# A decoder layer on one core: Y rows loaded by token halves, head values two to a PSUM bank, merged rows' low parts on VectorE, and three gate columns left at the first logits

## The chip, the cores and the metric

The kernel runs on one core of a Trainium2 chip. The metric is the device time of one execution in microseconds, lower is better; the time before is the median of three executions. TensorE (PE) multiplies matrices into PSUM banks of 128 x 512 float32 values; VectorE (DVE), ScalarE (ACT) and GpSimd (POOL) move and change data; SyncE (SP) issues most of the DMA transfers.

## The reference, cut to what matters

One layer, 1024 tokens, width 1024, eight heads of 64 in each of two attentions that run side by side. The change touches the sparse attention's output, the gated merge and the start of the output projection.

```python
x = x + 0.5 * swiglu(rms_norm(x, g_ffn1), w1_gate, w1_up, w1_down)      # inner width 2816
h = rms_norm(x, g_mix)
(c_q, k_a, v_a, k_idx, w_idx, q_b, k_b, v_b, gate_a, gate_b) = split(h @ w_in)
# A: sparse attention, each token attends to its 256 best keys by an indexer's score
logits = where(valid, q_a . k_a * HEAD_DIM ** -0.5, -inf)
p = softmax(logits)                                                     # per head
o_lat = p @ v_a                                                         # latent values, 128 wide
y_a = concat over heads of (o_lat @ w_uv[head])                         # value weights, 128 x 64 a head
# B: stick-breaking attention, causal, without softmax
y_b = (exp(log_sigmoid(z) + cumulated log_sigmoid(-z))) @ v_b
merged = sigmoid(gate_a) * (y_a @ w_o_a) + sigmoid(gate_b) * (y_b @ w_o_b)
x = x + merged @ w_out
x = x + 0.5 * swiglu(rms_norm(x, g_ffn2), w2_gate, w2_up, w2_down)
```

## The kernel before

Everything is float32. A product is made of three matmuls of a faster format (`mm3`, L306 to L310): each operand is split into a high part, a rounded copy made by ScalarE, and a low part, the rest, made by a subtraction on VectorE or POOL. Names ending in h and l (`uvh`, `uvl`, `wg7h`, `wout010l`) are such parts; `halve` (L375) puts the high part of a 128 x 512 piece into the first half of a tile and its low part into the second.

The two SwiGLU halves at the ends take most of the time and are not touched. Between them lies a part in which the order of TensorE's, VectorE's, ScalarE's and POOL's work is written out by a planner, `Weave`. Each piece of work is a generator that yields the engine it wants next and what it needs: tiles, marks (named events), free places in a ring of buffers, and a rank. `Weave.run` steps the piece that by a table of costs can begin first, and of those the one with the lowest rank. So a change in one piece moves others. SP's queue takes its transfers strictly in the order in which they were written. Behind the planner's part the order is set by the framework's scheduler.

The pieces that the change touches, in the planner's second stretch:

- `fillers` projects the columns of values, queries and keys, and then the sixteen 128-wide columns of the two gates, 48 matmuls `psf` a column, with weights `wg0` to `wg7` for the last eight. Before the last two but one column in its list it sets the mark "warm", for which `logits` waits. `gate_out` scales the results (with one more instruction on POOL if ScalarE's table is already that of the exponential) and writes them to memory.
- `sparse` loads the value weights (`uvraw`): POOL clears two tiles of 128 x 512, eight transfers of 128 x 64 fill them, ScalarE and POOL make `uvh` and `uvl`.
- `logits`, `logit_out` and `soft`: for each block of 128 queries and each head, TensorE's logits `psL`, VectorE's masking and maximum `mx` (L1907), ScalarE's exponential (L1919) and VectorE's division `e` (L1922). `latent_values` and `latent_products` turn e on TensorE (`pspT`, L1998) and multiply it with the latent values (`pso`).
- `head_values` multiplies pairs of 128-token blocks with the value weights: for four pairs of heads, six matmuls `psya` of 256 columns each, into a bank of the ring `fbank`; `ya_out` makes the parts `yah` (ScalarE, L2037) and `yal` (VectorE, L2039).
- `outputs` and `project`: B's output rows come back from memory in tiles of 128 x 1024 (`ybh0` to `ybh3` and `ybl0` to `ybl3`, 512 KB each) and are multiplied with `w_o_b` (`psob`); one wait stands for all eight tiles. The second token half of A's product (`psoa`) follows. `gate_load` brings the gates, `gated` and `merged` multiply (`o`, L2064 to L2078) and store. The eight Y_b tiles share a ring of 16 (`ht`) with other tiles.

Then, outside the planner: for the first token half A's product `psm` with gates and B's part loaded into tiles of the same ring of 16 (L2147, L2148: eight times two transfers of 256 KB), the product with `w_out` (`psout`, L308 to L310 with weights `wout000` and on), and between its halves `merged` (L2210), which loads the second token half's merged rows `m10` to `m17` and halves them, low parts on POOL (L378). The adds to the residual stream, `x` L2184, are on VectorE.

Of the kernel before, what the change touches and what calls it, by code (L numbers as in the profile page):

```python
# [21 lines left out]
PE, DVE, ACT, POOL, SP = "PE", "DVE", "Activation", "Pool", "SP"  # L22

P = 128
# [7 lines left out]
HD = 64  # L32
# [25 lines left out]
def f32(ap):  # L58
    return ap.bitcast(F32)
# [34 lines left out]
class Weave:  # L94
# [113 lines left out]
    def spawn(self, gen, rank=1, own=None):  # L208
        s = Stream(gen, rank, own or self.own)
        self.streams.append(s)  # L210
        self.step(s)
        return s
# [33 lines left out]
def trunk(ctx, tc, x, positions, g_ffn1, w1_gate, w1_up, w1_down, g_mix, w_in, g_cq, w_uq_a, w_q_idx,  # L246
          g_q_a, g_k_a, w_uv_a, w_o_a, w_o_b, w_out, g_ffn2, w2_gate, w2_up, w2_down, inv_freq, out):
    nc = tc.nc
# [15 lines left out]
    def ht(name, dt=F32R):  # L264
        return hpool[-1].tile([P, 1024], dt, tag="h", name=name, bufs=16)
# [40 lines left out]
    def mm3(ps, ah, al, bh, bl, first, last):  # L306

        nc.tensor.matmul(ps, ah, bh, start=first, stop=False)  # L308
        nc.tensor.matmul(ps, ah, bl, start=False, stop=False)  # L309
        nc.tensor.matmul(ps, al, bh, start=False, stop=last)  # L310
# [62 lines left out]
    HI, LO = slice(0, 512), slice(512, 1024)  # L373

    def halve(t, src, eng=None):  # L375

        nc.scalar.activation(t[:, HI], src, AF.Copy)
        (eng or nc.gpsimd).tensor_tensor(t[:, LO], src, f32(t[:, HI]), op=ALU.subtract)  # L378
        return t
# [398 lines left out]
    ybd = [dram.tile([512, S], F32, name=f"yb{p}d") for p in "hl"]  # L778
# [40 lines left out]
    with tc.tile_pool(name="ring1", bufs=1) as rpool, tc.tile_pool(name="s1", bufs=1) as spool, tc.tile_pool(name="ps1", bufs=1, space=PSUM) as psum:  # L819
        op, raw = ring(rpool)  # L820
        bank = banks(psum, fpsum)
        sums, pair = of(spool, "s", 5, 512), of(spool, "pair", 2, 512, F32R)
        with tc.tile_pool(name="t1", bufs=1, side="right") as tpool, tc.tile_pool(name="c1", bufs=1) as cpool:
            tt, ts = of(tpool, "t", 24, dt=F32R), of(tpool, "ts", 4, dt=F32R)
# [42 lines left out]
            def rows(t):  # L867
                xs.append(fp(tt if t > 3 else ts)(f"x{t}"))
                nc.sync.dma_start(xs[t], x[0, t * P:(t + 1) * P, :])
# [89 lines left out]
        h2, rows = [], []  # L959
# [31 lines left out]
        rows = normed(xs[0:4], "m0", sx)  # L991
# [36 lines left out]
    with ctxf, fp as fpool, psm as psum, tc.manual_schedule(  # L1028
# [174 lines left out]
        def fillers():  # L1203
            yield from proj_v(0)
            for n, (pr, (base, nh_, nl_, sc)) in enumerate(todo):
                if n == 4:
                    yield from proj_v(1)
                if not n % 2:
                    outs = []
                s = feed()  # L1210
                yield PE, s
                for half in range(2):
                    yield PE, fbank
                    ps, cols = yield from fproj(s.parts, half)
                    outs.append(spawn(qk_out(ps, pr, nh_, nl_, sc, cols)))
                give(*s.parts)
                if n % 2:
                    mark(f"qk{pr}", *outs, qkd["kl"], qkd["kh"], qkd["qh"], qkd["ql"])
            outs = []
            for g in gates:  # L1220
                if g == gates[-2]:
                    mark("warm")
                s = feed()
                yield PE, s
                for half in range(2):
                    yield PE, fbank, late(3)
                    ps, cols = yield from fproj(s.parts, half, lambda: late(3))
                    outs.append(spawn(gate_out(ps, g, cols)))
                give(*s.parts)
            mark("gates", *outs)  # L1230
# [638 lines left out]
        def sparse():  # L1869
            c = here["c"] = outputs_of[1] = place("sd", "right")  # L1870
            here["gate"], here["e"] = ring_of(c, "gate", 3, (P, 512)), ring_of(c, "e", 3)

            UV.extend((c("uvh", "uvh", 1, F32R), c("uvl", "uvl", 1, F32R)))
            raws = [here["gate"]("uvraw") for half in range(2)]
            mark("c")
            yield POOL
            for half, raw in enumerate(raws):
                nc.gpsimd.memset(raw, 0.0)
                for h in range(4):
                    nc.sync.dma_start(raw[:, h * P + h % 2 * HD:h * P + (h % 2 + 1) * HD], w_uv_a[0, 4 * half + h])  # L1880
            for half, raw in enumerate(raws):
                cols = slice(half * 512, half * 512 + 512)
                yield ACT, raw
                nc.scalar.activation(UV[0][:, cols], raw, AF.Copy)
                yield POOL, raw, UV[0]
                nc.gpsimd.tensor_tensor(UV[1][:, cols], raw, f32(UV[0][:, cols]), op=ALU.subtract)
                give(raw)
            mark("uv", UV[1])
# [115 lines left out]
            yield PE, *outs  # L2004
            give(*KV)

        ybh, ybl, yah, yal = [], [], [], []

        def head_values():
            yield PE, "gates"  # L2010
            yah.extend(ht(f"yah{p}") for p in range(4))
            yal.extend(ht(f"yal{p}") for p in range(4))
            yield PE, "uv"
            uvh, uvl = UV
            for n in range(NT // 2):
                i = blocks[2 * n] // 2 * 2
                yield PE, f"o{n}"
                cols = slice(i * P, (i + 2) * P)
                outs = []
                for pr in range(4):  # L2020
                    yield PE, fbank
                    bank = fbank("psya")
                    yp = bank[:, 0:256]
                    for e in range(2):
                        h = 2 * pr + e
                        oh, ol = (a[:, (h % 4) * 256:(h % 4 + 1) * 256] for a in OT[i // 2, h // 4])
                        hc = slice(h * P, (h + 1) * P)
                        mm3(yp, uvh[:, hc], uvl[:, hc], oh, ol, e == 0, e == 1)
                    outs.append(spawn(ya_out(bank, yah[pr], yal[pr], cols)))
                for g in range(2):  # L2030
                    give(*OT[i // 2, g])
                mark(f"ya{n}", *outs)

        def ya_out(bank, hi, lo, cols):
            yp = bank[:, 0:256]
            yield ACT, bank
            nc.scalar.activation(hi[:, cols], yp, AF.Copy)  # L2037
            yield DVE, bank, hi
            nc.vector.tensor_sub(lo[:, cols], yp, f32(hi[:, cols]))  # L2039
            give(bank)  # L2040
# [45 lines left out]
        def project(nm, rows, halves, outs):  # L2086

            for d in range(0, ND, 2):
                W = feed()
                yield PE, W  # L2090
                wh, wl = W.parts
                for e in range(2):
                    for half in halves:
                        yield PE, rows[-1][-1], fbank
                        cols = slice(half * 512, half * 512 + 512)
                        ps, r = fbank("ps" + nm), slice((d + e) * P, (d + e + 1) * P)
                        row, to = (ND + d + e, obd[r, cols]) if nm == "ob" else (d + e, md[r, :])
                        coming = spawn(gate_load(row, d + e, half, nm == "oa"))
                        for k in range(4):
                            c = slice((2 * k + e) * P, (2 * k + e + 1) * P)  # L2100
                            mm3(ps, wh[:, c], wl[:, c], rows[0][k][:, cols], rows[1][k][:, cols], k == 0, k == 3)
                            if k < 3:
                                yield PE
                        outs.append(spawn((merged if nm == "oa" else gated)(ps, coming, row, half, to)))
                    if nm == "ob":
                        mark(f"obd{d + e}", *outs[-len(halves):])
                give(*W.parts)

        def outputs():

            yield PE, "gates"
            ybh.extend(ht(f"ybh{p}") for p in range(4))
            ybl.extend(ht(f"ybl{p}") for p in range(4))
            yield SP, "o"
            for p in range(4):
                nc.sync.dma_start(f32(ybh[p]), ybd[0][p * P:(p + 1) * P, :])
                nc.sync.dma_start(f32(ybl[p]), ybd[1][p * P:(p + 1) * P, :])
            yield PE, "c"
            outs = []
            yield from project("ob", (ybh, ybl), range(2), outs)  # L2120
            yield PE, "ya2"
            yield from project("oa", (yah, yal), range(1, 2), outs)

        for g, rank in ((v_loads(), 0), (values(), 0), (sticks(), 1), (head_values(), 2), (latent_values(), 3), (logits(), 4),
                        (hidden_keys(), 1), (latent_queries(), 1), (outputs(), 6)):
# [11 lines left out]
    with tc.tile_pool(name="ring2", bufs=1) as rpool, tc.tile_pool(name="ps6", bufs=1, space=PSUM) as psum:  # L2137
        op, raw = ring(rpool)
        bank = banks(psum)
        with tc.tile_pool(name="m0", bufs=1) as mpool:  # L2140
# [70 lines left out]
            def merged():  # L2211
                for d in range(0, ND, 2):
                    m = raw(f"m1{d}r")
                    nc.sync.dma_start(m.rearrange("p (k f) -> p k f", k=2),
                                      md[d * P:(d + 2) * P, :].rearrange("(k p) f -> p k f", p=P))
                    M1.extend(halve(tt(f"m1{d + q}"), m[:, c]) for q, c in enumerate((HI, LO)))

            project(0, M0, x0, merged)
        sums = of(ctx3.enter_context(tc.tile_pool(name="s2", bufs=1)), "s", 7, 512)
# [76 lines left out]
```

## Time and profile before

| what | value |
| --- | --- |
| median of three executions | 2169.08 us (2166.69 to 2172.35) |
| the profiled execution: its time, its span | 2170.9 us, 2169.1 us |
| mean granted TensorE clock | 0.998 |
| TensorE, VectorE, ScalarE, POOL busy | 98%, 71%, 48%, 42% of the span |
| moved by DMA | 378.89 MB, 174 GB/s of HBM traffic over the span |

In the profile an idle time stands in brackets behind the instruction that it precedes, with what ended it. Two figures are not the same: an idle time is the gap between instructions as recorded, while TensorE's matmuls are issued every 0.23 us (512 columns) and overlap by about 0.16 us, so the delay from start to start is a little longer. The planner's second stretch ends where `psm` begins, at 1411.65 us.

### The profile page before, as it was taken

How to read it: one execution, taken by the hardware profiler on the slowest of the kernel's cores; microseconds unless marked ns; L12 is line 12 of the kernel's file. 1: busy time of each engine (PE TensorE's matmuls, PEld its weight loads, DVE VectorE, ACT ScalarE, POOL GpSimd, SP SyncE). 2: the span in 40 equal slices, each digit the busy share in tenths (PEclk: the TensorE clock that was granted, in tenths of full speed). 3: DMA queues.
4: the chain of work that ended last, by engine and by line, in shares of the span. 5: the costliest groups of instructions: out<-in, count | busy, mean ns of one | idle time of the engine just before them, and what ended most of it. 6: DMA issues, size and time to landing. Idle time of an engine off the chain costs nothing.

```text
span 2169.1 us, 30135 instructions
## 1 busy us (share of the span) xinstructions
PE 2129.0 (98%) x10308; PEld 1778.4 (82%) x10308; DVE 1537.0 (71%) x2610; ACT 1044.2 (48%) x1973; POOL 914.6 (42%) x738
## 2 busy tenths in 40 slices
PE   7999999999999999999999999999999999999999
PEld 6888888888889989788888788778888888888877
DVE  7776767678874599888885788644764646578685
ACT  6433343334454357988775566334432232323443
POOL 5555555523345443332211332364564555542223
PEclk9999999999999999999999999999999999999999
DMA  5587877497675343676544432665132323359755
GB/s 157 135 249 221 246 206 240 157 331 240 214 214 163 104 133 123 219 194 169 165 160 146 163 123 85 214 247 185 54 121 92 127 93 98 107 186 313 233 170 189
DMA packets 276890, 378.89 MB, mean 175 GB/s; under 512 B 39808, under 2 KB 165392, under 8 KB 276736
## 3 DMA queue, kind: packets, MB, share of 16 engines
q1 hardware_dynamic: 264704, 339.17, 50.2%
q0 software_dynamic: 12032, 37.79, 4.8%
q8 instruction: 81, 1.33, 0.3%
q14 instruction: 73, 0.60, 0.1%
HBM read 259.94 MB, written 116.95 MB: 174 GB/s over the span
## 4 chain that ended last, share of the span: by engine, by line
PE 84%; DVE 6%; issue 3%; ACT 3%; DMA 3%; POOL 1%; SPq 0%; ACTq 0%; DVEq 0%; POOLq 0%
PE p L737 6%; PE p L738 6%; PE p L736 6%; PE pa L499 4%; PE pa L497 3%; PE pa L498 3%; PE pc L497 3%; PE pc L499 3%; PE pc L498 3%; PE pd L497 3%; PE pd L499 3%; PE pd L498 3%; PE psf L308 3%; PE psf L310 3%; PE psf L309 3%
## 5 line engine op out<-in xcount | busy, mean ns | idle before, releaser
L1286 ACT ACTIVATE junka<-u,cand,sig 128x768 bf16<-128x768 f32 (+1 forms) x124 | 134.4, 1084 | 3.7 <-DVE cand L1278 2.3
L1727 DVE TENSOR_TENSOR_SCAN left<-left 128x640 f32<-128x640 f32 (+3 forms) x64 | 86.5, 1368 | 1.1 <-ACT left L1721 1.0
L859 ACT ACTIVATE swh<-swr 128x512 fp32r<-128x512 f32 x48 | 30.2, 629 | 117.3 <-issue 47.4
L860 DVE TENSOR_TENSOR swr<-swr,swh 128x512 f32<-128x512 f32 x48 | 43.6, 909 | 39.8 <-ACT swh L859 34.9
L1788 DVE TENSOR_TENSOR pt<-pspT,pt 128x512 fp32r<-128x512 f32 x72 | 46.7, 684 | 28.5 <-ACT pt L1782 28.3
L1200 POOL DMA_DIRECT2D gd<-evg x32 | 18.2, 569 | 101.8 <-ACT evg L1195 100.1
L1785 DVE SCALAR_TENSOR_TENSOR pt<-pstT,pt 128x512 fp32r<-128x512 f32 (+1 forms) x96 | 51.5, 547 | 13.6 <-ACT pt L1782 13.2
L640 ACT ACTIVATE b0u<-b0u 128x512 f32<-128x512 f32 x20 | 12.7, 633 | 99.0 <-DVE b0u L520 82.9
L1782 ACT ACTIVATE pt<-pspT 128x512 fp32r<-128x512 f32 x72 | 39.6, 596 | 38.7 <-PE pspT L1998 38.5
L1782 ACT ACTIVATE pt<-pstT 128x512 fp32r<-128x512 f32 (+1 forms) x96 | 46.4, 493 | 23.9 <-PE pstT L1842 21.7
L1919 ACT ACTIVATE e<-e,nm 128x768 f32<-128x768 f32 (+7 forms) x64 | 49.4, 775 | 13.3 <-DVE nm L1914 10.1
L1907 DVE CUSTOM_DVE_ANT_0 e<-psL,bias 128x512 f32<-128x512 f32 (+3 forms) x96 | 50.0, 550 | 5.7 <-PE psL L1944 5.6
L737 PE MATMUL p<-bT,bS 128*128 128x512 f32 x132 | 51.6, 391 | 0.8 <-DVE bT L378 0.8
L737 PE MATMUL p<-aT,aS 128*128 128x512 f32 x132 | 51.5, 390 | 0.9 <-DVE aT L378 0.9
L1640 DVE SCALAR_TENSOR_TENSOR u<-relu,WI,u 128x512 f32<-128x512 f32 (+1 forms) x70 | 49.2, 722 | 3.8 <-ACT relu L1633 2.7
L738 PE MATMUL p<-aT,aS 128*128 128x512 f32 x132 | 50.7, 389 | 0.0
L1633 ACT ACTIVATE relu<-psdot 128x512 f32<-128x512 f32 (+1 forms) x80 | 39.7, 519 | 22.7 <-DVE u L1640 13.3
L738 PE MATMUL p<-bT,bS 128*128 128x512 f32 x132 | 50.4, 389 | 0.0
L2069 POOL TENSOR_TENSOR o<-o,gate 128x512 f32<-128x512 f32 x16 | 21.0, 1315 | 62.2 <-ACT o L2064 62.1
L736 PE MATMUL p<-bT,bS 128*128 128x512 f32 x132 | 47.0, 389 | 0.0
L1842 PE MATMUL pstT<-ident,left 128*128 128x128 f32 x288 | 45.9, 272 | 0.0
L1721 ACT ACTIVATE left<-psz 128x512 f32<-128x512 f32 (+2 forms) x96 | 44.0, 501 | 2.5 <-PE psz L1750 2.1
(3046 smaller groups left out, 8219.3 us busy)
## 6 DMA issues: line engine op xcount, KB each, us to landing
aw<-in_w_down_dram SPq DMA_DIRECT2D x33, 512.0 KB, 5.1
bw<-in_w_down_dram SPq DMA_DIRECT2D x33, 512.0 KB, 4.9
swr<-in_w_in_dram SPq DMA_DIRECT2D x48, 256.0 KB, 6.0
a0r<-in_w_gate_dram SPq DMA_DIRECT2D x22, 512.0 KB, 7.7
a1r<-in_w_up_dram SPq DMA_DIRECT2D x22, 512.0 KB, 7.4
b0r<-in_w_gate_dram SPq DMA_DIRECT2D x22, 512.0 KB, 4.1
b1r<-in_w_up_dram SPq DMA_DIRECT2D x22, 512.0 KB, 3.8
x<-in_x_dram SPq DMA_DIRECT2D x16, 512.0 KB, 6.3
```

What stands on the lines that cost most here:

```text
L308: nc.tensor.matmul(ps, ah, bh, start=first, stop=False)
L309: nc.tensor.matmul(ps, ah, bl, start=False, stop=False)
L310: nc.tensor.matmul(ps, al, bh, start=False, stop=last)
L497: nc.tensor.matmul(ps, a[:, c], b[k][:, HI], start=start and k == 0, stop=False, skip_group_check=True)
L498: nc.tensor.matmul(ps, a[:, c], b[k][:, LO], start=False, stop=False, skip_group_check=True)
L499: ins = nc.tensor.matmul(ps, a[:, l], b[k][:, HI], start=False, stop=k == 3, skip_group_check=True)
L736: nc.tensor.matmul(ps[q][m], S[:, h], T[:, HI], start=p == 0, stop=False)
L737: nc.tensor.matmul(ps[q][m], S[:, h], T[:, LO], start=False, stop=False)
L738: nc.tensor.matmul(ps[q][m], S[:, l], T[:, HI], start=False, stop=p == last)
L1286: nc.scalar.activation(junks[1][:, 0:(i + 1) * P], score[i], AF.Sign, scale=sig[:, b:b + 1], bias=cand.bitcast(F32)[:, b:b + 1], accum_out ...
L1727: nc.vector.tensor_tensor_scan(back, back, back, 1.0, op0=ALU.mult, op1=ALU.bypass)
L1782: nc.scalar.activation(pt[:, off:512], tp[:, off:512], AF.Copy, bias=-less)
```

## The change

It has five parts, none of which changes what is computed or how many matmuls there are.

1. The mark "warm" is set one gate column earlier, so three gate columns are left when the logits may begin.
2. The value weights come in four transfers of 128 x 2 x 64.
3. Two pairs of heads share a PSUM bank, each with its half of the columns; the bank is given free when both are done.
4. Y_b comes in eight tiles, each with the high and the low part of one token half of 128 rows, in sixteen transfers of 256 KB, the second token half first; a product waits for its own half only and takes half 1 before half 0.
5. The low parts of `m10` to `m17` are made by VectorE.

```diff
-                if g == gates[-2]:
+                if g == gates[-3]:
                     mark("warm")
...
-                for h in range(4):
-                    nc.sync.dma_start(raw[:, h * P + h % 2 * HD:h * P + (h % 2 + 1) * HD], w_uv_a[0, 4 * half + h])
+                for e in range(2):
+                    at = e * (P + HD)
+                    nc.sync.dma_start(raw.rearrange("p (g x) -> p g x", g=2)[:, :, at:at + HD],
+                                      w_uv_a[0, 4 * half + e:4 * half + 4:2].rearrange("g p d -> p g d"))
...
                 for pr in range(4):
-                    yield PE, fbank
-                    bank = fbank("psya")
-                    yp = bank[:, 0:256]
+                    if pr % 2 == 0:
+                        yield PE, fbank
+                        bank = fbank("psya", 2)
+                    yp = bank[:, pr % 2 * 256:pr % 2 * 256 + 256]
...
                     for half in halves:
-                        yield PE, rows[-1][-1], fbank
+                        high, low = rows(half)
+                        yield PE, low[-1], fbank
...
-            ybh.extend(ht(f"ybh{p}") for p in range(4))
-            ybl.extend(ht(f"ybl{p}") for p in range(4))
+            order_ = [(half, p) for half in (1, 0) for p in range(4)]
+            yb.update((at, ht(f"yb{at[0]}{at[1]}")) for at in order_)
             yield SP, "o"
-            for p in range(4):
-                nc.sync.dma_start(f32(ybh[p]), ybd[0][p * P:(p + 1) * P, :])
-                nc.sync.dma_start(f32(ybl[p]), ybd[1][p * P:(p + 1) * P, :])
+            for half, p in order_:
+                for n, part in ((0, HI), (1, LO)):
+                    nc.sync.dma_start(f32(yb[half, p][:, part]),
+                                      ybd[n][p * P:(p + 1) * P, half * 512:half * 512 + 512])
...
-                    M1.extend(halve(tt(f"m1{d + q}"), m[:, c]) for q, c in enumerate((HI, LO)))
+                    M1.extend(halve(tt(f"m1{d + q}"), m[:, c], nc.vector) for q, c in enumerate((HI, LO)))
```

What it moves, at three places. First SP's queue at the start of the value weights and Y_b, before and then after. `gate` is a gate's rows for B's merge, `qs` the queries of a block, `ob4r` and `ob6r` weights.

```order
L2056 DMA gate<-gd 128x512
L2116 DMA ybh_12155<-ybhd 128x1024
L2117 DMA ybl_12159<-ybld 128x1024
L1880 DMA uvraw<-in_w_uv_a_dram 128x64 x8
L1381 DMA qs<-qad 128x1024
L2116 DMA ybh_12156<-ybhd 128x1024
L2117 DMA ybl_12160<-ybld 128x1024
```

```order
L2058 DMA gate<-gd 128x512
L1881 DMA uvraw<-in_w_uv_a_dram 128x2x64 x4
L1381 DMA qs<-qad 128x1024
L2120 DMA yb_12186<-ybhd 128x512
L2120 DMA yb_12186<-ybld 128x512
L2120 DMA yb_12187<-ybhd 128x512
L2120 DMA yb_12187<-ybld 128x512
```

The value weights and a block's queries now stand ahead of all Y_b loads, of which sixteen half-size ones follow one another.

Second TensorE at the end of the last gate column (`wg7`), before and then after; `psL` are logits, `pspT` the turned softmax of the first long block.

```order
L308 MATMUL psf_11971<-mhi7_5582,wg7h_11716 128x512
L309 MATMUL psf_11971<-mlo7_5590,wg7h_11716 128x512
L310 MATMUL psf_11971<-mhi7_5582,wg7l_11717 128x512
L1943 MATMUL psL_12097<-kkh_10678,qs_10975 128x512
L1944 MATMUL psL_12097<-kkl_10685,qs_10975 128x512
L1943 MATMUL psL_12100<-kkh_10678,qs_10975 128x256
L1944 MATMUL psL_12100<-kkl_10685,qs_10975 128x256
L1943 MATMUL psL_12108<-kkh_10678,qs_10975 128x512
L1944 MATMUL psL_12108<-kkl_10685,qs_10975 128x512
L1943 MATMUL psL_12117<-kkh_10678,qs_10975 128x256
L1944 MATMUL psL_12117<-kkl_10685,qs_10975 128x256
L1998 MATMUL pspT_12128<-ident_71,e_11790 128x128
```

```order
L308 MATMUL psf_12040<-mhi6_5581,wg7h_11781 128x512
L309 MATMUL psf_12040<-mlo6_5589,wg7h_11781 128x512
L310 MATMUL psf_12040<-mhi6_5581,wg7l_11782 128x512
L308 MATMUL psf_12040<-mhi7_5582,wg7h_11781 128x512
L309 MATMUL psf_12040<-mlo7_5590,wg7h_11781 128x512
L310 MATMUL psf_12040<-mhi7_5582,wg7l_11782 128x512
L2000 MATMUL pspT_12097<-ident_71,e_11727 128x128
L2000 MATMUL pspT_12097<-ident_71,e_11974 128x128
L2000 MATMUL pspT_12097<-ident_71,e_11983 128x128
```

Before, 18 matmuls of `wg7` and eight of logits stood between the logits ahead and the transposes; now 30 matmuls of `wg7` stand there, and those eight logits were moved forward into the gate columns.

Third POOL between the first two quarters of the product with `w_out`, before and then after.

```order
L297 TENSOR_TENSOR wout006l_14727<-wout006r_14723,wout006h_14725 128x1024
L378 TENSOR_TENSOR m10_14763<-m10r_14761,m10_14763 128x512
L378 TENSOR_TENSOR m11_14766<-m10r_14761,m11_14766 128x512
L378 TENSOR_TENSOR m12_14771<-m12r_14769,m12_14771 128x512
L378 TENSOR_TENSOR m13_14774<-m12r_14769,m13_14774 128x512
L378 TENSOR_TENSOR m14_14779<-m14r_14777,m14_14779 128x512
L378 TENSOR_TENSOR m15_14782<-m14r_14777,m15_14782 128x512
L378 TENSOR_TENSOR m16_14787<-m16r_14785,m16_14787 128x512
L378 TENSOR_TENSOR m17_14790<-m16r_14785,m17_14790 128x512
L297 TENSOR_TENSOR wout010l_14801<-wout010r_14797,wout010h_14799 128x1024
```

```order
L297 TENSOR_TENSOR wout002l_14665<-wout002r_14661,wout002h_14663 128x1024
L297 TENSOR_TENSOR wout004l_14695<-wout004r_14691,wout004h_14693 128x1024
L297 TENSOR_TENSOR wout006l_14725<-wout006r_14721,wout006h_14723 128x1024
L297 TENSOR_TENSOR wout010l_14799<-wout010r_14795,wout010h_14797 128x1024
L297 TENSOR_TENSOR wout012l_14829<-wout012r_14825,wout012h_14827 128x1024
```

The eight subtractions now stand on VectorE between the last row of the first half (`m07`) and the first adds `x` to the residual stream; on SP the load of `wout010r` moved ahead of the last load of `m`.

More of the change, by code (lines that the diff above doesn't have):

```diff
@@ L2005, in latent_values @@
             give(*KV)
-        ybh, ybl, yah, yal = [], [], [], []
+        yah, yal, yb = [], [], {}
         def head_values():
@@ L2028, in head_values @@
                         mm3(yp, uvh[:, hc], uvl[:, hc], oh, ol, e == 0, e == 1)
-                    outs.append(spawn(ya_out(bank, yah[pr], yal[pr], cols)))
+                    outs.append(spawn(ya_out(bank, yp, yah[pr], yal[pr], cols)))
                 for g in range(2):
@@ L2032, in head_values, with ya_out @@
                 mark(f"ya{n}", *outs)
-        def ya_out(bank, hi, lo, cols):
-            yp = bank[:, 0:256]
+        def ya_out(bank, yp, hi, lo, cols):
             yield ACT, bank
@@ L2093, in project @@
                     for half in halves:
-                        yield PE, rows[-1][-1], fbank
+                        high, low = rows(half)
+                        yield PE, low[-1], fbank
+                        ps, r = fbank("ps" + nm), slice((d + e) * P, (d + e + 1) * P)
                         cols = slice(half * 512, half * 512 + 512)
-                        ps, r = fbank("ps" + nm), slice((d + e) * P, (d + e + 1) * P)
                         row, to = (ND + d + e, obd[r, cols]) if nm == "ob" else (d + e, md[r, :])
@@ L2100, in project @@
                             c = slice((2 * k + e) * P, (2 * k + e + 1) * P)
-                            mm3(ps, wh[:, c], wl[:, c], rows[0][k][:, cols], rows[1][k][:, cols], k == 0, k == 3)
+                            mm3(ps, wh[:, c], wl[:, c], high[k], low[k], k == 0, k == 3)
                             if k < 3:
@@ L2111, in outputs @@
             yield PE, "gates"
-            ybh.extend(ht(f"ybh{p}") for p in range(4))
-            ybl.extend(ht(f"ybl{p}") for p in range(4))
+            order_ = [(half, p) for half in (1, 0) for p in range(4)]
+            yb.update((at, ht(f"yb{at[0]}{at[1]}")) for at in order_)
             yield SP, "o"
-            for p in range(4):
-                nc.sync.dma_start(f32(ybh[p]), ybd[0][p * P:(p + 1) * P, :])
-                nc.sync.dma_start(f32(ybl[p]), ybd[1][p * P:(p + 1) * P, :])
+            for half, p in order_:
+                for n, part in ((0, HI), (1, LO)):
+                    nc.sync.dma_start(f32(yb[half, p][:, part]),
+                                      ybd[n][p * P:(p + 1) * P, half * 512:half * 512 + 512])
             yield PE, "c"
             outs = []
-            yield from project("ob", (ybh, ybl), range(2), outs)
+            yield from project("ob", lambda half: [[yb[half, p][:, part] for p in range(4)] for part in (HI, LO)], (1, 0), outs)
             yield PE, "ya2"
-            yield from project("oa", (yah, yal), range(1, 2), outs)
+            yield from project("oa", lambda half: [[t[:, LO] for t in y] for y in (yah, yal)], (1,), outs)
         for g, rank in ((v_loads(), 0), (values(), 0), (sticks(), 1), (head_values(), 2), (latent_values(), 3), (logits(), 4),
```

## The prediction

> **What bounds the kernel.** I read the page first (busy table, chain by engine), then the groups of TensorE's instructions from 1100 to 1500 us with the idle time before them, since every edit lies there, and then the timeline around each idle time.
>
> ```profile
> span 2169.1 us, 30135 instructions
> PE 2129.0 (98%) x10308; PEld 1778.4 (82%) x10308; DVE 1537.0 (71%) x2610; ACT 1044.2 (48%) x1973; POOL 914.6 (42%) x738
> PE 84%; DVE 6%; issue 3%; ACT 3%; DMA 3%; POOL 1%; SPq 0%; ACTq 0%; DVEq 0%; POOLq 0%
> ...
> L1998 PE MATMUL pspT<-ident,e 128*128 128x128 f32 x288 | 38.7, 273 | 3.0 <-DVE e L1922 2.9
> L1943 PE MATMUL psL<-kkh,qs 128*128 128x512 f32 (+2 forms) x96 | 35.1, 373 | 1.8 <-DVE mx L1907 1.8
> L308 PE MATMUL psya<-oh,uvh 128*128 128x256 f32 x32 | 9.8, 308 | 4.5 <-DVE o L2078 2.5 <-DVE yal L2039 2.0
> ```
>
> TensorE is busy 98% of the span and carries 84% of the chain, and the change takes no matmul away. So all that can be won is TensorE's idle time in this stretch, and the halved clock that follows some of it. Five waits over 1.5 us lie here: e and mx in one place, yal, o, and a fifth in W_out.
>
> **First logits and value weights: the gate column left over, four loads for eight, their place ahead of Y_b.** The rows are SP's queue, ScalarE, TensorE and VectorE in order of time; then a row of SP's waits, and two windows (the last three columns: granted clock, DMA share, GB/s).
>
> ```profile
> 1202.84 0.32 SPq L2116 DMA_DIRECT2D ybh<-ybhd  x1
> 1204.01 5.44 SPq L1880 DMA_DIRECT2D uvraw<-in_w_uv_a_dram  x8
> DMA to landing us min/median/max: 1.8/4.0/5.4
> 1210.31 0.63 ACT L1884 ACTIVATE uvh<-uvraw 128x512 fp32r<-128x512 f32 x1 [2.27 <-DMA uvraw<-in_w_uv_a_dram]
> 1215.19 0.39 PE L1943 MATMUL psL<-kkh,qs 128*128 128x256 f32 x1 [1.62 <-DVE mx L1907]
> 1215.25 2.76 DVE L1922 TENSOR_SCALAR e<-e,ri 128x768 f32<-128x768 f32 x1
> 1218.06 0.77 PE L1998 MATMUL pspT<-ident,e 128*128 128x128 f32 x5 [2.04 <-DVE e L1922]
> ...
> SPq L1880 <- DMA ybl<-ybld: 1.3, 1, 1.3
> ...
> 1219.31:1222.72 3.41, 3.41 (x10) 2.62 (x10) 3.37 (x12) 2.00 (x5) 0.08 (x1) 0.50 0.99 310
> 1366.08:1369.50 3.42, 3.42 (x12) 2.94 (x13) 1.09 (x4) 0.38 (x1) 0.00 (x0) 0.50 0.41 143
> ```
>
> The eight small value-weight loads stand behind Y_b's first loads on SP, and one waits for such a load to land. ScalarE sits 2.27 us before the copy uvh, and the softmax's exponentials are queued behind that copy; VectorE's e comes late, and TensorE waits 1.62 + 2.04 = 3.66 us. Then its clock is halved for 3.41 us, which costs half of that, 1.7. In the changed order four loads are issued, ahead of all Y_b loads: at 5.44/8 = 0.68 us each that is 2.7 us, from about 1203.9 to 1206.6, and by the 1.8 to 4.0 us to landing they are there at 1208.4 to 1210.6, at best 1.9 us before the copy now starts and at worst no earlier. Beyond that, all of the first logits stand before the last 30 gate matmuls on TensorE, where eight logit matmuls now stand between gates and transposes; the last gate column covers VectorE's e. I therefore take nearly all of it: 3.7 + 1.7 removed, 0.6 left over. The ends: 0 (the copy is as late, and the exponentials behind it) and 5.4. Moving the gate column by itself costs nothing on TensorE, since the same 48 matmuls are issued later as filler; two more gate halves are scaled on POOL, which is 42% busy.
>
> **Two head pairs to a bank.** TensorE's third pair waits for a bank that VectorE's low part still reads.
>
> ```profile
> 1365.98 0.51 PE L308 MATMUL psya<-oh,uvh 128*128 128x256 f32 x1 [1.74 <-DVE yal L2039]
> 1364.17 0.67 ACT L2037 ACTIVATE yah<-psya 128x256 fp32r<-128x256 f32 x2
> 1365.51 0.75 DVE L2039 TENSOR_TENSOR yal<-psya,yah 128x256 fp32r<-128x256 f32 x2
> ```
>
> With two pairs to a bank the four pairs of a block need two banks of the ring where they needed four; the 1.74 us and the halved clock behind it (3.42 us at 0.50, so 1.7) go: 3.4 removed. Against that, the first pair's copy can start only behind the second pair's six matmuls, and a bank is held for two copies and two low parts, 0.67 + 0.75 = 1.4 us of evacuation. Eight blocks could each show a part of that; most stand before other work. I take 0.8 in all, ends 0 and, with 0.4 in each of eight, 3.2.
>
> The Trainium skill speaks against this edit: its page "PSUM — Partial Sum Buffer", section "PSUM bank collisions raise a hardware error", wants banks guarded as a whole, not by address, so a copy from one half of a bank may not run beside matmuls into the other. By it the upper end of the range above would be the likelier.
>
> **Tail: Y_b by token halves, gate loads of the merge.** The rows are the windows at 1375 us, two pieces of the chain, the wait it ends in, and the next stage's first wait; then two pieces of the chain that give the pace of transposes and matmuls, and Y_b's loads and first use.
>
> ```profile
> 1375.00:1400.00 25.00, 22.27 (x114) 18.54 (x113) 13.18 (x32) 10.19 (x23) 8.62 (x7) 1.00 1.01 358
> 1385.85 7.32 DMA gate<-gd
> 1393.29 0.70 DVE o L2078
> who waited for it (us, times):
>   DVE o L2078: 3.1, 1
> 1411.65 0.47 PE L308 MATMUL psm<-yah,woa0h 128*128 128x512 f32 x1 [0.87 <-DVE o L2078]
> ...
> 1194.98 0.55 PE pspT L1998 x5
> 1195.76 0.23 PE psf L309
> DMA to landing us min/median/max: 4.2/5.3/8.4
> L308 PE MATMUL psob<-ybh,ob0h x16: 387/394/477, 1232.2 to 1267.7; 128*128 128x512 f32 x16
> ```
>
> Today the merge's sixteen gate and obd loads are all issued when the last Y_b tile comes free, and fill the DMA engines (share 1.01); a gate load behind them takes 7.32 us, VectorE's o waits 3.1, and TensorE 2.5 (the psya group's column above). By the new order TensorE uses up the Y_b tiles before the last of the A outputs, half 1 well before half 0, so these loads go out earlier and in two lots: 2.5 removed. The start of psm then waits for the low part of the last head pair rather than for o; I put that at 1.4 for 0.87 (two low parts instead of one), so 0.5 added.
>
> The Y_b loads themselves move the same 4 MB. Half 1 is eight loads of 256 KB, issued within about 8 x 0.43 = 3.4 us and, by the 8.4 us of the slowest larger load, landed 11.8 us after the first at worst. In the new order TensorE has some 13.7 us of work from the first tile's release to its first psob: the rest of the last gate half (21 matmuls by 0.23, 4.8 us), then 22 logit and output matmuls of 512 columns by 0.23, 10 of 256 by about half of that and 24 transposes by 0.55/5 = 0.11, 8.9 us. Hidden, with 2 us to spare at worst and 4 to 5 likely. A load later than that costs TensorE microsecond for microsecond.
>
> **Merged rows' low parts.** POOL does eight m before the low part that TensorE waits for.
>
> ```profile
> 1443.72 2.53 POOL L378 TENSOR_TENSOR m<-m10r,m 128x512 fp32r<-128x512 f32 x2
> 1453.13 1.06 ACT L295 ACTIVATE wout010h<-wout010r 128x1024 fp32r<-128x1024 f32 x1 [0.18 <-DMA wout010r<-in_w_out_dram]
> 1456.16 2.34 POOL L297 TENSOR_TENSOR wout010l<-wout010r,wout010h 128x1024 fp32r<-128x1024 f32 x1
> 1458.56 0.50 PE L309 MATMUL psout<-wout010l,m 128*128 128x512 f32 x1 [2.20 <-POOL wout010l L297]
> 1437.39 0.69 DVE L378 TENSOR_TENSOR m<-gate,m 128x512 fp32r<-128x512 f32 x1
> 1439.81 1.69 DVE L378 TENSOR_TENSOR m<-gate,m 128x512 fp32r<-128x512 f32 x1 [1.13 <-ACT m L377]
> 1451.41 0.69 DVE L2184 TENSOR_TENSOR x<-x,psout 128x512 f32<-128x512 f32 x1 [9.92 <-PE psout L310]
> 1475.67 0.69 DVE L2184 TENSOR_TENSOR x<-x,psout 128x512 f32<-128x512 f32 x1 [19.49 <-PE psout L310]
> ```
>
> Without the eight m (pairs of 2.53 us, 10.1 in all) POOL is free when ScalarE's high part wout010h ends, now at 1454.2, and wout010l would end at 1456.5 even if its weights landed no earlier; TensorE needs it at 1458.56 - 2.20 = 1456.4. The weight load is also issued ahead of the last m load now. So the 2.20 us go. On VectorE the eight cost 0.69 to 1.69 us each, 5.5 to 13.5, in the 9.92 us of idle time before the adds x, some of them behind those adds' due time; the next 19.49 us of idle time take the delay. Nothing in TensorE's queue waits for these adds before 1475 us. Ends: 0 and 2.2 removed.
>
> The long 1.69 us are of an instruction with two inputs in SBUF beside POOL's. The Trainium skill says the same in "SBUF — State Buffer", section "Who interferes with whom": such a VectorE instruction shares a port with a reading POOL one, and one of the two blocks. By it the last m could hold wout010l in turn, and half of the 2.2 would come back.
>
> **VectorE and the small waits.** The planner's stretch behind the first logits:
>
> ```profile
> 1225.00:1250.00 25.00, 24.84 (x143) 20.99 (x144) 22.04 (x74) 15.29 (x36) 4.67 (x6) 1.00 0.15 46
> 1250.00:1275.00 25.00, 24.16 (x139) 20.87 (x138) 22.48 (x87) 15.79 (x44) 7.08 (x6) 1.00 0.39 126
> 1275.00:1300.00 25.00, 24.32 (x130) 19.95 (x129) 20.84 (x54) 16.01 (x30) 8.88 (x9) 1.00 0.38 120
> ```
>
> VectorE works 65.4 of 75 us here (the third of the busy pairs). With TensorE's early waits gone the same softmax has to fit into less time, and gate matmuls that filled gaps are used up sooner. I add 2.0 for new waits here and 0.8 where the Y_b filler has run out near the end of the attention; ends 0 and two waits like the 2.04 one with its halved clock, 7.5. The small waits that stand now stay in the sum as they are.
>
> **Sum.** Removed: 5.4 + 3.4 + 2.5 + 2.2 = 13.5. Added: 0.6 + 0.8 + 0.5 + 2.0 + 0.8 = 4.7. Gain 8.8; the profiled execution took 2170.9 us, 1.8 more than its span, so it would be 2162.1. The three timed runs have a median of 2169.08, 1.8 below that execution, so 2160.3 as a median.
>
> **Rivals.**
> - VectorE becomes the bound behind the first logits. For it: 22.48 of 25 us. Against it: the last gate column stands before the transposes. One transpose wait costs 2.04 + 1.7 = 3.7; with two instead of the 2.0 taken the gain is 3.3, 2166. From three it is no gain at all, and from five, 8.8 - (18.7 - 2.0) = -7.9, it ends slower, at 2177.
> - The value weights are as late as now (upper landing 1210.6), and ScalarE's exponentials behind them: 5.4 - 0.6 = 4.8 not won, 2165.
> - Two pairs to a bank do not do what they are for: a wait of the old size at another pair, 3.4 not won, 2163.7.
> - Y_b late: 4 us beyond the margin take 4 of the 8.8, 2164.5.
> - The halved clock is not the waits' doing: it followed the 2.04 and the 1.74 us, but not the 2.5 at 1394 (granted clock 1.00 in that window). Were both stretches to stay, 3.4 would not be won, 2163.7. In the Trainium skill ("TensorE: Matmul & The Clock Gate", "What's actually happening") the clock falls after an idle window of some 3.4 us; by that rule neither wait here is long enough. The trace's two stretches have that length and begin 1.3 us or less after the waits, so I keep the cause.
>
> **Numbers.** Chances: the forecast 0.60; VectorE 0.15 for two waits, 0.05 for five; late weights 0.06; the bank 0.06; Y_b 0.03; the clock 0.05. A measurement of this kernel tells 0.3%, 6.5 us, from no change. The forecast is faster; the bank and clock cases (gain 5.4) lie about the border and go half to faster: 0.60 + 0.055 = 0.65. Same: 0.15 + 0.06 + 0.03 + 0.055 = 0.30. Slower 0.05. The range runs from 2152 (all 13.5 and some of the small waits won, 1 to 2 us added) to 2167, which takes in all cases but five VectorE waits. The likeliest case's own range is 2155 to 2163.
>
> **What would show it.** Right: no wait of psL or pspT over 1 us near 1215 and no 0.50 window behind it; uvraw landing before 1209; no psya wait on yal or o over 1 us; psout on wout010l without a wait, and x adds with less idle time. Wrong: pspT or psL waiting for VectorE's e or mx between 1225 and 1300, each with a half-rate window; a psob waiting for a Y_b load; wout010l still behind 1456.

## The result and the profile after

| | before | changed |
| --- | --- | --- |
| median of six runs | 2170.14 us (2166.69 to 2174.05) | 2155.58 us (2154.83 to 2157.59) |
| span of the profiled execution | 2169.1 us | 2153.1 us |

The ratio is 0.9933, with a 95% interval of 0.9921 to 0.9946: 14.6 us faster. The forecast was 2160.3, 8.8 us faster. The page of the changed kernel, then all of TensorE's waits over 0.2 us from 1150 to 1500 us (wait in total, times, longest).

```profile
span 2153.1 us, 30147 instructions
PE 2122.8 (99%) x10308; PEld 1775.2 (82%) x10308; DVE 1550.2 (72%) x2618; ACT 1041.4 (48%) x1973; POOL 907.1 (42%) x732
...
PE psm L308 <- DVE yal L2041: 1.6, 1, 1.6
PE psout L309 <- POOL wout010l L297: 0.4, 1, 0.4
PE pso L1980 <- ACT pt L1782: 0.4, 1, 0.4
PE psL L1945 <- DVE mx L1909: 0.3, 1, 0.3
PE psya L308 <- ACT o L2066: 0.3, 1, 0.3
PE pso L1982 <- DVE pt L1788: 0.2, 1, 0.2
```

Of the five waits over 1.5 us none is left in its place; the only long one is psm's, at the seam to the next stage, which the change lengthened. The next two lines are the same 400 us of before and of the changed kernel, the last three columns being granted clock, DMA share and GB/s.

```profile
1100.00:1500.00 400.00, 386.96 (x1918) 322.83 (x1918) 265.37 (x719) 209.48 (x400) 138.73 (x120) 0.99 0.48 165
```

```profile
1100.00:1500.00 400.00, 396.77 (x2003) 333.98 (x2002) 288.59 (x740) 216.10 (x416) 135.71 (x115) 1.00 0.51 171
```

TensorE is idle for 3.2 us where it was idle for 13.0, and no stretch with a halved clock is left. By first starts: from the first wg4 matmul to the first psm it took 1411.65 - 1156.24 = 255.4 us and now 1397.14 - 1155.54 = 241.6, 13.8 less; from psm to the second half's first psout 67.9 and now 66.1, 1.8 less. The second half begins 16.3 us earlier; the remaining 0.7 lies ahead of wg4, where nothing was changed, and in the other executions below wg4 begins anywhere from 1155.3 to 1157.2 us.

At the first logits the changed kernel shows SP, ScalarE, VectorE and the window:

```profile
1204.39 1.92 SPq L1881 DMA_DIRECT2D uvraw<-in_w_uv_a_dram  x4
1208.64 0.63 ACT L1886 ACTIVATE uvh<-uvraw 128x512 fp32r<-128x512 f32 x1 [0.71 <-DMA uvraw<-in_w_uv_a_dram]
1210.42 0.65 DVE L1924 TENSOR_SCALAR e<-e,ri 128x768 f32<-128x768 f32 x1
1200.00:1225.00 25.00, 25.00 (x134) 21.23 (x133) 18.21 (x62) 14.41 (x29) 9.40 (x11) 1.00 0.80 279
```

The weights are copied 1.7 us earlier, the division e takes 0.65 us for 2.76, and TensorE does not stop. Which of the two did it the page does not say; the experiments do.

At the merged rows, POOL, TensorE, VectorE and ScalarE of the changed kernel:

```profile
1439.09 2.41 POOL L297 TENSOR_TENSOR wout010l<-wout010r,wout010h 128x1024 fp32r<-128x1024 f32 x1 [9.78 <-ACT wout010h L295]
1441.56 0.50 PE L309 MATMUL psout<-wout010l,m 128*128 128x512 f32 x1 [0.39 <-POOL wout010l L297]
1436.74 1.29 DVE L378 TENSOR_TENSOR m<-m14r,m 128x512 fp32r<-128x512 f32 x2 [5.07 <-ACT m L377]
1439.95 4.91 DVE L378 TENSOR_TENSOR m<-m16r,m 128x512 fp32r<-128x512 f32 x2 [1.92 <-ACT m L377]
1459.34 0.69 DVE L2188 TENSOR_TENSOR x<-x,psout 128x512 f32<-128x512 f32 x1 [12.10 <-PE psout L310]
1437.90 1.06 ACT L295 ACTIVATE wout010h<-wout010r 128x1024 fp32r<-128x1024 f32 x1 [0.68 <-DMA wout010r<-in_w_out_dram]
```

POOL now waits 9.78 us for the weights; what is left of TensorE's wait, 0.39, is the weights' landing. VectorE's last two subtractions take 4.91 us beside wout010l and wout012l where the two ahead took 1.29, and VectorE still has 12.1 us of idle time behind them.

### The profile page after: what moved, and what is told of

The parts are those of the page before. It is cut to its first block, busy times and chain, and to the rows that moved or that the text cites. A ratio compares the mean times of both kernels' runs of the same rounds, so it can differ in the third digit from the quotient of the medians.

```text
span 2153.1 us, 30147 instructions
## 1 busy us (share of the span) xinstructions
PE 2122.8 (99%) x10308; PEld 1775.2 (82%) x10308; DVE 1550.2 (72%) x2618; ACT 1041.4 (48%) x1973; POOL 907.1 (42%) x732
## 5 line engine op out<-in xcount | busy, mean ns | idle before, releaser
L377 ACT ACTIVATE bT<-bt 128x512 fp32r<-128x512 f32 x44 | 26.5, 625 | 39.6 <-PE p L738 32.2
```

## The experiments

Theory: each of the five waits has its own local cause, the one named in the prediction, and the parts add up. Rivals: the parts work through the order that the planner makes of them; or an engine that was said to be near its limit is not. Ten kernels have one part of the change alone on the kernel before (only) or the changed kernel without one part (less); two test single causes.

| part | alone, ratio to before | taken out of the changed kernel, ratio to before |
| --- | --- | --- |
| mark "warm" | 0.9978 (0.9968 to 0.9987) | 0.9943 (0.9931 to 0.9956) |
| four value-weight loads | 0.9996 (0.9987 to 1.0005) | 0.9935 (0.9922 to 0.9947) |
| two pairs to a bank | 0.9973 (0.9962 to 0.9984) | 0.9963 (0.9951 to 0.9974) |
| Y_b by token halves | 0.9974 (0.9963 to 0.9986) | 0.9946 (0.9935 to 0.9958) |
| low parts on VectorE | 0.9988 (0.9979 to 0.9996) | 0.9951 (0.9938 to 0.9963) |
| all five | 0.9933 (0.9921 to 0.9946) | |

### The mark

```diff
-                if g == gates[-2]:
+                if g == gates[-3]:
```

> Before with the one changed mark: three gate columns are left at the first logits. Eight value-weight loads stay eight, but the planner now puts them ahead of all Y_b loads, and 30 gate matmuls stand before the first long transposes. Theory (each wait has its own local cause): the 3.7 us of waits at the first logits and the halved clock behind them (1.7 us) go, the yal, o and wout010l waits stay: -5.4 us, ratio 0.9975, about 2164.7. Rival 1 (the filler that is left over helps every later wait): -12 us, 0.9945. Rival 2 (the mark only shifts work): within 2 us of before.

2165.89 us, 0.9978: near the local theory's number, but partly by luck. Some of TensorE's waits, 1150 to 1500 us, then the division e that TensorE waited for before, POOL beside it, and TensorE:

```profile
PE psya L308 <- DVE yal L2039: 4.7, 4, 1.7
PE psL L1943 <- DVE mx L1907: 1.5, 2, 1.2
PE pspT L1998 <- DVE e L1922: 0.8, 1, 0.8
...
1210.22 2.20 DVE L1922 TENSOR_SCALAR e<-e,ri 128x768 f32<-128x768 f32 x1
1209.46 2.54 POOL L1886 TENSOR_TENSOR uvl<-uvraw,uvh 128x512 fp32r<-128x512 f32 x2
1211.75 0.39 PE L310 MATMUL psf<-mhi,wg7l 128*128 128x512 f32 x1
1211.98 1.26 PE L1998 MATMUL pspT<-ident,e 128*128 128x128 f32 x8
```

The long wait on e is gone and the halved clock behind it too. The division is still long here, 2.20 us beside POOL's uvl, but TensorE works on the last gate column until 1211.98 us and on other heads' transposes behind it, and shows no gap. Yet the waits of psya on yal grew from 2.0 us in two places to 4.7 in four, and a stretch of halved clock now follows the wait on wout010l, while the 2.5 us on o are gone: the number is about the theory's, the waits are not. In the changed kernel none of psya's waits on yal is left.

> The changed kernel with the mark where it was (two gate columns left); four value-weight loads, but three Y_b loads stand ahead of them on SP again. Against the changed kernel at 2155.6. Theory: the waits at the first logits come back in part, 1 to 3.7 us, with or without a halved clock: 2157 to 2161, ratio to before 0.994 to 0.996. Rival (the four loads alone repaired it): 2155.6, 0.9933. Rival (filler): waits on e and mx between 1225 and 1300 us come back as well: 2163 and more.

2157.85 us, 0.9943. The wait on e is back with its 2.0 us and a halved clock, though the four value-weight loads were issued within 1.6 us; no wait on mx over 0.35. The interval overlaps that of the whole change; the trace decides here.

### The value weights

```diff
-                for h in range(4):
-                    nc.sync.dma_start(raw[:, h * P + h % 2 * HD:h * P + (h % 2 + 1) * HD], w_uv_a[0, 4 * half + h])
+                for e in range(2):
...
```

> Before with four value-weight loads for eight; TensorE's order is word for word that of before, and one pair of Y_b loads still stands ahead on SP. Theory: uvraw issues in 2 us for 5.4 and lands some 1.5 to 2.5 us earlier, ScalarE's exponentials are not held behind the copy, the waits of 3.7 us shrink to under 2 and the halved clock may go: -2 to -5 us, ratio 0.9985. Rival (the eight logits between gates and transposes are the cause, not the loads): waits stay at 3.7, ratio 1.000.

2170.6 us, 0.9996. First the loads on SP and their landing (min, median, max), then VectorE and TensorE.

```profile
L1881 SPq DMA_DIRECT2D uvraw<-in_w_uv_a_dram x4: 383/438/1162, 1204.5 to 1206.7; - x4
DMA to landing us min/median/max: 4.0/4.8/5.4
...
1215.27 2.74 DVE L1924 TENSOR_SCALAR e<-e,ri 128x768 f32<-128x768 f32 x1
1218.06 1.33 PE L2000 MATMUL pspT<-ident,e 128*128 128x128 f32 x5 [2.02 <-DVE e L1924]
```

The issues end 2.4 us earlier (1206.7 for 1209.1), but each lands later, median 4.8 for 4.0 us behind the Y_b loads, so the weights are hardly sooner there. TensorE's wait on e is what it was. That left the prediction's cause of the wait on e without support, and pointed to another: the division takes 2.74 us, not 0.64. In the kernel before it began at 1215.25 us; POOL of before:

```profile
1215.24 2.35 POOL L1091 TENSOR_TENSOR ob2l<-ob2r,ob2h 128x1024 fp32r<-128x1024 f32 x1 [0.46 <-ACT ob2h L1089]
```

The two began within 0.01 us of each other, and the division ended 0.42 us after ob2l. So I moved ob2l alone.

```diff
-                yield POOL, raw, wh
+                yield POOL, raw, wh, "pp010" if nm == "ob2" else None
```

> Before with one thing moved: POOL's low part ob2l (2.35 us) stands behind the gate scaling and its store in POOL's queue, no longer ahead of them; the value weights are as late as before. Theory now (port): VectorE's division e took 2.76 us for 0.64 because it ran beside ob2l. So e takes under 1.2 us, TensorE's 2.04 us wait on it falls under 0.6, the halved clock behind it goes; the 1.6 us wait on mx ahead stays: -2 to -3.7 us, ratio 0.9983 to 0.9991. Rival (my prediction's: the late value weights hold the exponentials): wait on e stays near 2 us, ratio 1.000.

2166.26 us, 0.9985 (0.9975 to 0.9994). ScalarE, VectorE, POOL and TensorE:

```profile
1211.18 0.63 ACT L1884 ACTIVATE uvh<-uvraw 128x512 fp32r<-128x512 f32 x1 [2.25 <-DMA uvraw<-in_w_uv_a_dram]
1216.14 0.62 DVE L1922 TENSOR_SCALAR e<-e,ri 128x768 f32<-128x768 f32 x1
1218.17 2.41 POOL L1091 TENSOR_TENSOR ob2l<-ob2r,ob2h 128x1024 fp32r<-128x1024 f32 x1
1216.09 0.39 PE L1943 MATMUL psL<-kkh,qs 128*128 128x256 f32 x1 [1.61 <-DVE mx L1907]
```

The value weights are as late as ever (ScalarE waits 2.25 us for them), yet the division takes 0.62, TensorE no longer waits on e, and no halved clock follows here. So the 2.04 us were POOL's doing. The wait on mx stays at 1.61, and to that one the prediction's cause fits. In the seven kernels with the mark in its old place, ScalarE's wait for the value weights and TensorE's wait on mx grow together: 0.98 and 0.35 us, 1.03 and 0.39, 1.77 and 1.14, 1.84 and 1.20, 2.06 and 1.41, 2.25 and 1.61, and 2.27 and 1.62 in the kernel before, always 0.63 to 0.65 apart.

> The changed kernel with eight value-weight loads for four; TensorE's order is the same and the loads stand ahead of Y_b's in both. Theory (not the loads but what lies beside the division decides): the eight land 1 to 2 us later, no wait of TensorE follows: 2155.6, ratio to before 0.9933. Rival (loads): ScalarE's copy holds an exponential, TensorE waits 1 us and more for e or mx near 1212: 2157 and more, 0.994.

2155.49 us, 0.9935; the same waits as the changed kernel to 0.05 us. With the loads ahead of Y_b on SP, four or eight of them make no difference.

### Two head pairs to a bank

```diff
-                    yield PE, fbank
-                    bank = fbank("psya")
+                    if pr % 2 == 0:
+                        yield PE, fbank
+                        bank = fbank("psya", 2)
```

> Before with two head pairs to a bank. Theory (local cause): the 1.74 us psya wait on yal and its halved clock go, the first-logits waits and wout010l stay; -3.4 us, ratio 0.9984, 2166.7. Rival (order): the planner lets psoa start earlier and Y_b end earlier in this kernel, so that the 2.5 us wait on o in the jam of gate loads goes too: -5.9 us, 0.9973.

2165.04 us, 0.9973; three of its waits:

```profile
PE pspT L1998 <- DVE e L1922: 2.0, 1, 2.0
PE psya L308 <- DVE o L2078: 1.8, 1, 1.8
PE psya L308 <- ACT o L2064: 0.3, 1, 0.3
```

The wait of psya on yal is gone everywhere, with the halved clock behind it, and the new waits are two of 0.3 us, the one shown and one on mx. The kernel wins more than the 3.4 us of that wait: the waits of 0.83 us on e and 0.60 on pt between 1257 and 1288 went too, in another order of the planner's. The number is the rival's by luck, for its reason did not hold: although the merge's gate loads left SP from 1348 to 1358 us, not from 1373 to 1385, the wait on o stayed at 1.8.

> The changed kernel with one head pair to a bank. Theory: a psya wait on yal of 1 to 2 us comes back where six or twelve psya stand in a row, with a halved clock behind it if it is that long: 2157 to 2159.5, ratio to before 0.994 to 0.995. Rival (order): psob and psya keep each other apart, and the wait on o at the end is back as well since psoa ends with 48 in a row and gate loads jam: 2162, 0.9963. Third: no difference.

2161.9 us, 0.9963. The most dear of the five to take out, and the only one whose interval stands clear of the whole change's. The wait and the window behind it:

```profile
1364.66 0.58 PE L308 MATMUL psya<-oh,uvh 128*128 128x256 f32 x1 [2.90 <-DVE yal L2041]
1364.20:1371.00 6.80, 6.34 (x22) 5.37 (x23) 2.35 (x9) 1.11 (x4) 0.00 (x0) 0.53 0.25 86
```

Here the wait is longer than before, and the clock stays halved for 6.8 us, of which the first 0.9 still fall into the wait. The other 6.0 cost half of their length: 2.9 + 3.0 us, most of the 6.3 that the kernel loses.

### Y_b by token halves

```diff
-            for p in range(4):
-                nc.sync.dma_start(f32(ybh[p]), ybd[0][p * P:(p + 1) * P, :])
-                nc.sync.dma_start(f32(ybl[p]), ybd[1][p * P:(p + 1) * P, :])
+            for half, p in order_:
...
```

> Before with Y_b by token halves, half 1 first. Theory: the merge's gate loads leave in two lots, the 2.5 us wait on o goes: -2.5 us, ratio 0.9988; the first-logits waits and wout010l stay, and the value-weight loads stand behind three Y_b loads. Rival: psob starts three transposes earlier (it is the only filler there), and a psob waits for a Y_b load by up to 4 us, or the value weights land later: 0 to +4 us, 1.000 to 1.002.

2165.23 us, 0.9974, better than either theory. Some of its waits:

```profile
PE psya L308 <- DVE yal L2039: 2.1, 3, 1.0
PE pspT L1998 <- DVE e L1922: 2.0, 1, 2.0
PE psob L308 <- DVE yal L2039: 0.7, 1, 0.7
```

The wait on o is gone and no psob waited for a load, although psob starts 10 us earlier. The planner, with Y_b's first half in hand sooner, also took the eighteen head-value matmuls in a row apart that made the 1.74 us wait: yal now costs 2.1 us in three pieces. No stretch of halved clock was granted in this execution at all, in spite of two waits over 2 us. That is most of the gain: TensorE is idle for 11.1 us from 1150 to 1500 us where it was idle for 13.0, 1.9 us less, and the two stretches of before had cost 3.4. So the number owes more to luck with the clock than to the tail.

> The changed kernel with Y_b in whole rows of 1024, eight loads. Theory: the jam of gate loads comes back at the end of the attention, TensorE waits 1 to 2.5 us for o: 2156.6 to 2158, ratio to before 0.994. Rival (the earlier end of Y_b came from the bank and mark edits): no wait on o over 0.5 us, 2155.6, 0.9933.

2158.51 us, 0.9946. No wait on o behind gate loads; instead 0.7 on yah, 0.86 on yal and 1.5 on mx. So neither text was right: with the other four parts in place the jam does not come back. TensorE's idle time is 1.2 us more than in the changed kernel (4.4 for 3.2); most of the loss of some 3 us, which is not clear of noise since the two intervals overlap, is not found in it.

### Merged rows' low parts

```diff
-                    M1.extend(halve(tt(f"m1{d + q}"), m[:, c]) for q, c in enumerate((HI, LO)))
+                    M1.extend(halve(tt(f"m1{d + q}"), m[:, c], nc.vector) for q, c in enumerate((HI, LO)))
```

> Before with the low parts of m10 to m17 on VectorE and nothing else. Theory: the wait of 2.2 us on wout010l shrinks to 0.4 or less, the x adds take the delay unseen: -1.8 us, ratio 0.9992, and the other waits as before. Rival (port): VectorE's m and POOL's wout010l hold one another up, the wait stays over 1 us: ratio 0.9996 to 1.000.

2167.16 us, 0.9988. The wait on wout010l is 0.47 us, near the theory's 0.4.

> The changed kernel with the low parts of m10 to m17 on POOL as before. Theory: TensorE waits 2.2 to 2.9 us for wout010l where it waits 0.39 now, and nothing else moves: +2 to +2.5 us, 2157.8, ratio to before 0.9944. Rival (VectorE and POOL hold one another up in the changed kernel): under +1 us.

2159.12 us, 0.9951. The wait, and the window behind it:

```profile
1444.99 0.50 PE L309 MATMUL psout<-wout010l,m 128*128 128x512 f32 x1 [2.06 <-POOL wout010l L297]
1445.80:1449.20 3.40, 3.40 (x9) 2.63 (x8) 0.00 (x0) 0.57 (x1) 1.47 (x1) 0.50 1.05 389
```

All other waits are as in the changed kernel. The wait came back by 1.7 us and was followed by a halved clock, 1.7 more: 3.4 of the 3.5 us.

### How near VectorE is to being the bound

```diff
-            yield ACT, ps, evr
+            yield DVE, ps, evr
             o = f32(evr("o"))
-            nc.scalar.activation(o, ps, AF.Copy)
+            nc.vector.tensor_copy(o, ps)
```

> The changed kernel with the copies of B's sixteen products out of PSUM on VectorE instead of ScalarE: 16 x 0.69 = 11 us more on VectorE between 1220 and 1360 us. Prediction's term (VectorE is the bound there): new waits of TensorE on VectorE, +4 us and more, 2160, ratio 0.9953. Rival (VectorE's idle time and the planner's new order take it): TensorE waits under 1.5 us more, within 1.5 us of 2155.6, 0.9933 to 0.994.

2160.8 us, 0.9962: 5.2 us slower than the changed kernel. Some of its waits, and its fullest window:

```profile
PE psob L308 <- DVE yal L2041: 1.6, 1, 1.6
PE pso L1980 <- DVE ol L1961: 1.1, 1, 1.1
PE pso L1982 <- DVE pt L1788: 0.9, 1, 0.9
PE psL L1945 <- DVE mx L1909: 0.8, 1, 0.8
PE pspT L2000 <- DVE e L1924: 0.6, 1, 0.6
1325.00:1350.00 25.00, 23.02 (x123) 18.52 (x122) 24.14 (x64) 15.48 (x31) 6.15 (x5) 1.00 0.73 247
```

Of 11 us more work on VectorE, 4.6 come out as waits of TensorE (7.8 us in all for 3.2). So VectorE is close to being the bound here; how close the change itself comes, no run shows.

## Why the prediction was right, and where its size was off

The sign and the place of the gain were right; the forecast gain of 8.8 us was 5.8 short.

- First logits. Forecast 5.4 removed, 0.6 left; measured 5.4 removed (1.62 + 2.04 and the clock), nothing left. The size held; the cause held for one of the two waits. The 1.62 us on mx go with ScalarE's wait for the value weights, as the prediction has it. But it laid e's lateness on these loads too, and hold_ob2l showed that the 2.04 us and the clock loss were a division of 0.64 us held to 2.76 beside ob2l on POOL. The 2.76 stood in a row that the prediction quoted; it was read as "late", not as "long". What repaired it in the changed kernel was the mark: with the mark alone the wait on e went, with the mark taken out it came back, with four loads alone it stayed. The mark does not keep the division short: in four of the seven kernels that have it the division takes 2.20 to 2.47 us beside uvl. The gate column left over covers it, and that step the prediction had right.
- Two pairs to a bank. Forecast 3.4 removed and 0.8 added; measured 3.4 and 0.28. A bank that is held for both pairs is copied later, and TensorE saw 0.28 us of that once.
- Tail. Forecast 2.5 removed, 0.5 added; measured 2.5 and 1.63 - 0.87 = 0.76. The gate loads of the merge left SP from 1327 to 1348 us, as the order promised; but since the wait on o survived early loads in one experiment and stayed away in less_yb, the loads' time is not the whole cause. What else there is was not tried. No psob waited for a Y_b load.
- Merged rows. Forecast 2.2, measured 1.8. The 0.39 left is the weights' landing. VectorE and POOL did hold one another up, but on VectorE's side and not, as the prediction feared, on wout010l: 4.91 us for two subtractions that take 1.29 alone, and 2.41 for wout010l, which took 2.34 before. The 4.91 fell into VectorE's idle time.
- VectorE and the small waits. This is the term that was mis-sized. Forecast 2.8 us added and the small waits kept; measured 0.32 + 0.36 + 0.24 = 0.9 added, and the small waits of before (0.16, 0.83, 0.04, 0.60, 0.22: 1.85 us) were gone. The fear was not empty, as gated_dve showed, but the windows of the changed kernel have VectorE at 18.88, 23.36 and 19.05 of 25 us from 1225 to 1300 where it had 22.04, 22.48 and 20.84: with the mark alone the first of the three is 18.50. So the earlier mark seems to spread VectorE's work over a longer time; that was not tested by itself.

Against the forecast these terms come to 0.6 + 0.5 - 0.3 - 0.4 + 1.9 + 1.85 = 4.2 of the 5.8. The measured idle times make 14.95 - 1.96 = 13.0 us of the 15.6 between wg4 and the second half. From start to start a wait costs TensorE about 0.17 us more than its idle time (1.79 for the 1.62 us on mx), and there are eight fewer of them (fourteen before and six now, the ones under 0.15 us counted), 1.4 us; 1.2 us were not assigned.

Whether the parts add up, the times do not tell. Alone they win 4.8, 0.9, 5.9, 5.6 and 2.6 us (from the ratios and 2170), 19.8 in all, together 14.6; but each of the five is uncertain by about 2 us, so the difference of 5.2 is about as large as its own uncertainty. Taken out one at a time they cost 15.8 in all. The traces show one overlap: bank and Y_b each remove the wait of 1.74 us on yal, one by giving banks, the other by moving the matmuls. And they show how much is clock: from 1150 to 1500 us the parts alone save 2.8, 0.9, 3.6, 1.9 and 2.5 us of TensorE's idle time, 11.7 in all, and together 9.8. The local theory is right for ob2l, for the bank as taken out, and for the merged rows; with the mark alone and with Y_b alone other waits moved as well, and halved clock came or went at waits that no edit had touched (at yal in only_m1, at wout010l in only_warm).

The rival of the halved clock fell: with the waits the stretches went, and the 3.4 us were won.

## What to carry to other kernels

Before a wait is laid on what came late, look at whether the instruction it ends in is longer than its equals: a division of 2.76 us among others of 0.64 names a neighbour, not a load. Then ask whether the repair removes the cause or only covers it: the division is still long in four of the seven kernels with the mark. Where a planner writes the order, an edit also moves waits elsewhere, so take parts out of the whole as well as adding them. And price a stall of TensorE near 2 us with the halved clock that may follow it, since that can cost as much as the stall.

## What the runs showed of the hardware

In the fourteen profiled executions TensorE had 23 waits of 1.7 to 2.9 us between 1206 and 1466 us. At twelve of them the granted clock was 0.50 for a time, beginning at most 0.9 us before and 1.5 us after the wait's end; it was below 0.99 nowhere else there, and not at waits of 1.63 us or less. Ten stretches lasted 3.4 us and two 6.8 (in only_uv and less_bank). While it works in them TensorE loses half of the time: 1.7 us, but 1.4 once and 3.0 twice where the stretch began before the wait had ended.

The wait's length alone does not decide. The same wait between the same matmuls (yal, 1.74 or 1.75 us) was followed by a stretch in three kernels and not in two. Where one execution has several stretches, they begin whole multiples of 3.413 us apart: 43 in the kernel before (1219.31 and 1366.08 us), 44 and 27 in only_uv (1217.17, 1367.36 and 1459.52). If windows of that length are laid by these times, or by the clock's fall at the end of the execution where no stretch was granted, the wait on yal lies in one window in the three kernels and across two in the other two. The first row is that window of only_uv, ahead of a stretch; the others are the two windows of only_m1, where none followed. Behind the length stands TensorE's busy time: it is idle for 1.74 us in the first row, 0.40 and 1.44 in the others.

```profile
1363.95:1367.36 3.41, 1.67 (x12) 1.28 (x12) 3.16 (x13) 2.71 (x8) 2.12 (x2) 1.00 0.10 29
1359.83:1363.24 3.41, 3.01 (x19) 2.15 (x18) 3.20 (x11) 3.41 (x11) 1.25 (x1) 1.00 0.01 2
1363.24:1366.65 3.41, 1.97 (x11) 1.77 (x12) 2.59 (x9) 1.38 (x5) 0.87 (x2) 1.00 0.41 154
```

In all fourteen executions, from 1150 to 1500 us, no window at full rate with up to 1.63 us of idle time was followed by halved clock, all nine with 1.95 or more were, and of the seven from 1.70 to 1.89 three were. The two long stretches are those whose first window still held 0.86 and 0.89 us of the wait; 0.67 in only_m1 made none longer. The longest wait, 2.93 us in only_yb, lay across two windows with 1.34 and 1.58 us of idle time and cost no clock. The Trainium skill's page "TensorE: Matmul & The Clock Gate" ("What's actually happening") gives a free-running window of 3413 ns, which agrees with the lengths and with the spacing; that the clock falls "after ≥1 idle window" does not agree, since about half a window of idle time was enough here.
